# Mixing's value, gate, projection and gated-unit matmuls with activations stationary and 512 weight columns moving

## The chip, the cores and the metric

The kernel runs on one core of one Trainium2 chip. The metric is the device time of one execution in microseconds (us): the median of the runs shown. The span of a profile goes from its first to its last instruction. TensorE multiplies a stationary tile (at most 128 x 128, brought in by a weight load) with a moving tile that streams through it column by column; the result lies in PSUM, which has 8 banks of 128 partitions x 512 float32. VectorE (DVE), ScalarE (ACT) and GpSimd (POOL) do the elementwise work. SyncE (SP) issues the weight transfers.

## The reference

Two layers of a decoder trunk on 256 tokens of width 1024. Each layer is a feed-forward block, a token mixing block and a second feed-forward block, each behind an RMS norm with a modulation (shift, scale, gate) computed from a conditioning vector. The change touches the mixing block alone:

```python
def mixing(h, w_in, ..., w_glu, w_attn_proj, w_out):
    proj = h @ w_in                                   # queries, keys, values, u, gates
    qkv, u, gates = jnp.split(proj, [QKV_COLS, QKV_COLS + SSM_WIDTH], axis=-1)
    ...                                               # o: 24 heads of windowed attention, merged
    y_attn = o.reshape(Bsz, S, ATTN_OUT) @ w_attn_proj
    y_ssm = s5_branch(u, ..., w_glu)                  # scans, gelu, then the gated unit: ga * sigmoid(gb)
    g_attn, g_ssm = jnp.split(jax.nn.sigmoid(gates), 2, axis=-1)
    return (g_attn * y_attn + g_ssm * y_ssm) @ w_out
```

Widths: the values have 1536 columns, the gates 2048, `w_attn_proj` is 512 x 1024, `w_glu` is 512 x 2048, `w_out` 1024 x 1024.

## The kernel before

**Precision.** Every large product is made of three matmuls in the one-pass format `float32r`: each operand is split into a high part and the rest, and `mm3` (line 200) adds high weight times low activation, high times high and low times high into the same PSUM tile. The weights are split on the chip: `split_one` (line 146) takes 1024 columns of a raw weight buffer, ScalarE casts them to the high part `whi` (line 163) and VectorE subtracts to get the low part `wlo` (line 164). Such a piece is called a half; it holds eight 128 x 128 weight tiles. Seven halves can be ready at once (`NHB`), so each cast waits until TensorE has finished with the half seven before it. SyncE reads the raw weights in units of two halves, in a fixed order that `plan_units` and `pack_layer` (line 1238) set; `half` (line 177) hands the next half to the code.

**Layout.** In nearly all products the weight tile is stationary, and the 256 tokens of an activation chunk move: the result has output channels on partitions and tokens along the row. A half is then 8 x 3 = 24 matmuls with 256 moving columns. The values are made the other way round already (`v_quad`, line 1101): the 128 tokens of one token tile are stationary and 256 weight columns move, so the result has tokens on partitions, as attention needs it.

**Mixing** (`mix_sub`, line 866) runs in this order: four column tiles for `u` and two of the first query tiles (`first_block`); query and key pair 0; values for heads 0 to 3 of each group (`v_quad(0)`); pair 1; `v_quad(1)`; pairs 2 and 3 (`qk_pair`); the gates (tiles `gt`, then a tanh on ScalarE into `th`, line 1160); the attention projection (`ap`, line 1167, merged into `th` at line 1168); the gated unit (`gb` and `ga`, line 1177), whose result is merged with the gates in four steps (tanh at line 1180, three VectorE operations at lines 1181 to 1183) and split into `hh` and `hl` (line 1188); and the output projection (`mo`, lines 1200 and 1208), which takes the merged chunks k = 0 to 7 as they come: for its first four column tiles the loop over k is outside. These merges are done for two channel chunks at a time, four times.

**Order.** After each half the code calls `tock` (line 935), which counts slots and emits what `at` put on the slot: the attention of head pair p begins at slot `X0[p]` and goes on in steps of one slot, the 16 state tiles of the scans are spread over slots 5 to 55, and four of the slots prepare the activation `yh`, `yl` of the gated unit. The order on SyncE, GpSimd and ScalarE is that of the code; the order on TensorE and VectorE inside mixing is set when the kernel is built, by a planner that estimates when each instruction can begin. At run time each engine goes through its own list in order.

Of the kernel before, what the change touches and what calls it, by code (L numbers as in the profile page):

```python
# [63 lines left out]
def plan_units():  # L64
    """Order in which the units of weights are read: ('w', i) or ('a', i)."""
# [37 lines left out]
def trunk(ctx, tc, xT, cv, par, ssmp, cst, emat, tbl, wada, wpk, bmat, cmat, out):  # L103
# [37 lines left out]
    def take_ada():  # L141
        """Modulation units whose turn it is."""
# [42 lines left out]
    def several(n):  # L185
        """Halves that are read together."""
# [13 lines left out]
    def mm3(ps, wh, wl, hh, hl, start, stop):  # L200
        T.matmul(ps, lhsT=wh, rhs=hl, start=start, stop=False)  # L201
        T.matmul(ps, lhsT=wh, rhs=hh, start=False, stop=False)  # L202
        T.matmul(ps, lhsT=wl, rhs=hh, start=False, stop=stop)  # L203
# [31 lines left out]
    def ada_unit():  # L235
        """256 columns of silu(c) @ w_ada, one column per partition and element."""
# [57 lines left out]
    def soon(fn):  # L294
        """fn, with its instructions ahead of those that are emitted up to SOON earlier."""
# [16 lines left out]
    def rstd_start():  # L312
        """1 / sqrt(mean of squares + eps), tokens on partitions."""
# [17 lines left out]
    def rstd_spread(ys):  # L331
        """The same on every partition, in PSUM."""
# [10 lines left out]
    def h_tiles(r, scale, shift, hh, hl):  # L343
        """scale * x * r + shift in two parts, chunk by chunk; the chunks take turns in how much of it
        the scalar engine does."""
# [9 lines left out]
        for k in range(KC):  # L355
            hh.append(base.tile([128, S], F32R, name=f"hh{k}", tag=f"hh{k}"))
            hl.append(base.tile([128, S], F32R, name=f"hl{k}", tag=f"hl{k}"))
            b = shift[:, k:k + 1]
            if k % 2:
                A.activation(out=hh[k], in_=t, func=AF.Identity, bias=b)  # L360
            else:
                A.activation(out=t, in_=t, func=AF.Identity, scale=scale[:, k:k + 1], bias=b)
                A.copy(out=hh[k], in_=t)
            n = first(k + 1) if k + 1 < KC else None
            if k % 2:
                stt(hl[k], t, b, hh[k], AD, SU)
            else:
                tt(hl[k], t, hh[k], SU)
# [133 lines left out]
    def table_side(l, pool):  # L502
        """Cosine and sine of each state's angle over time, for the scans of layer l."""
# [27 lines left out]
    def gate_of(sub):  # L531
        """Half the gate."""
# [71 lines left out]
    def first_block(nx, sj, rj):  # L604
        """Five column tiles of a sublayer's input projection. They read scale * x; the rest read the
        normed chunks, which are made meanwhile. What comes back: the banks, 1 / rms, the normed chunks."""
# [5 lines left out]
        def mm(j, w, k):  # L612
            mm3(pss[j][:, :S + 2], w[0][:, k, :], w[1][:, k, :], z[:, k, 0, :], z[:, k, 1, :], k == 0, k == KC - 1)

        hh, hl = [], []
# [13 lines left out]
        for j in range(4):  # L629
            for k in range(5, KC):  # L630
                mm(j, hs[j], k)
            if j == rj:
# [3 lines left out]
                ht = h_tiles(rs, scale, shift, hh, hl)  # L636
# [12 lines left out]
        return pss, rs, hh, hl  # L649

    def first_block_whole(nx, sub):
        """The same for four column tiles, in plain float32."""
        scale, shift, z = nx
        us = [("w", first[sub] + j) for j in range(2)]
        ws = [raw.pop(u).rearrange("p (a b) -> p a b", b=128) for u in us]
        look()
        pss = [bank("b1") for _ in range(4)]

        def mms(ks):
            for j in range(4):  # L660
                for k in ks:
                    T.matmul(pss[j][:, :S + 2], lhsT=ws[j // 2][:, 8 * (j % 2) + k, :], rhs=z[:, k, :],
                             start=k == 0, stop=k == KC - 1)
                if ks[0] == 0 and j == 1:
                    stat_mm()
                    stat["ys"] = rstd_start()
                if ks[0] > 0 and j % 2:
                    finish(us[j // 2])
                    take_ada()

        mms(range(5))
        rps = rstd_spread(stat["ys"])
        rs = tmp.tile([128, S], F32, name="rs", tag="sqa", bufs=1)
        A.copy(out=rs, in_=rps)
        hh, hl = [], []
        for k in h_tiles(rs, scale, shift, hh, hl):
            pass
        mms(range(5, KC))
        look()
        return pss, rs, hh, hl  # L680
# [39 lines left out]
        # bias of each head by distance, for each kind of block of keys: [pq + pk] is that of query  # L720
        # 127 - pq and key pk of the block
# [661 lines left out]
```

## Time and profile before

| what | value |
|---|---|
| median of 3 runs | 1365.01 us (1364.72 to 1365.94) |
| span of the profiled execution | 1361.8 us |
| own time of the profiled execution | not given apart from the span; the median lies 3.2 us above the span |
| TensorE (PE) busy | 1322.1 us, 97% of the span |
| VectorE (DVE) busy | 1098.3 us, 81% |
| ScalarE (ACT) busy | 757.2 us, 56% |
| GpSimd (POOL) busy | 292.6 us, 21% |
| mean granted TensorE clock | 0.993 of 2.4 GHz |

In the rows, PE is a matmul and PEld a weight load. Both are pipelined: the length of one is longer than the time from one start to the next, so the rate of a stream is read from the starts. PEclk is the granted TensorE clock as a share of 2.4 GHz. Inside a group, x is the number of instructions, then come the busy time in us and the mean length of one in ns, and after the second bar the idle time of that engine just before them with what ended it.

### The profile page before, as it was taken

The numbers are of one execution on the slowest core, as the hardware profiler recorded it, in microseconds if no ns is written. First come the engines' busy times: TensorE is split into PE (matmuls) and PEld (weight loads), VectorE is DVE, ScalarE is ACT, GpSimd is POOL, SyncE is SP. The second block draws the span as 40 slices with busy tenths as digits, with TensorE's granted clock in tenths as the row PEclk, the third lists the DMA queues.
The fourth block names the chain that finished last, engine by engine and source line by source line (L and its number), as shares of the span: only waits on it lengthen the run. The fifth ranks groups of instructions, "written<-read, shape, count | busy, mean of one in ns | idle before, by whom it ended". The sixth has DMA issues, their size and how long they took to land.

```text
span 1361.8 us, 26855 instructions
## 1 busy us (share of the span) xinstructions
PE 1322.1 (97%) x11018; PEld 1279.4 (94%) x11018; DVE 1098.3 (81%) x1757; ACT 757.2 (56%) x1162; POOL 292.6 (21%) x356
## 2 busy tenths in 40 slices
PE   4996999999999999999999999999999999999997
PEld 2996999998988999999999999999889999999997
DVE  8866997889899879998769888679889887876552
ACT  5634795645565456677646444454565645654441
POOL 5889691100000000877300000010000000000000
PEclk9997999999999999999999999999999999999999
DMA  9775997556665645998837988656555463586540
GB/s 356 297 289 175 369 347 274 187 193 207 219 234 219 217 153 170 347 370 321 279 124 291 351 316 333 247 174 227 173 199 198 163 220 128 182 307 217 186 155 32
DMA packets 48837, 321.60 MB, mean 236 GB/s; under 512 B 6048, under 2 KB 6432, under 8 KB 12746
## 3 DMA queue, kind: packets, MB, share of 16 engines
q1 hardware_dynamic: 41704, 296.24, 59.8%
q0 software_dynamic: 7008, 23.64, 5.4%
q8 instruction: 86, 1.41, 0.4%
q14 instruction: 37, 0.30, 0.1%
q10 hardware_dynamic: 2, 0.00, 0.0%
HBM read 310.38 MB, written 9.48 MB: 235 GB/s over the span
## 4 chain that ended last, share of the span: by engine, by line
PE 86%; POOL 6%; DVE 3%; issue 2%; ACT 1%; DMA 1%; DVEq 0%; POOLq 0%; ACTq 0%
PE pc L203 8%; PE pc L201 8%; PE pc L202 8%; PE fo L201 6%; PE fo L202 6%; PE fo L203 6%; PE qk L201 4%; PE qk L202 3%; PE qk L203 3%; PE gt L201 3%; PE gt L202 2%; PE gt L203 2%; PE b L201 2%; PE bu L949 2%; PE b L203 2%; PE b L202 2%
## 5 line engine op out<-in xcount | busy, mean ns | idle before, releaser
L164 DVE TENSOR_TENSOR wlo<-raw,whi 128x1024 fp32r<-128x1024 f32 x416 | 515.5, 1257 | 93.2 <-ACT whi L163 92.3
L163 ACT CAST whi<-raw 128x1024 fp32r<-128x1024 f32 x416 | 427.0, 1047 | 220.2 <-PE fo L202 71.3
L201 PE MATMUL pc<-hl,whi 128*128 128x256 f32 x1200 | 338.4, 282 | 8.7 <-ACT whi L163 8.7
L203 PE MATMUL pc<-hh,wlo 128*128 128x256 f32 x1200 | 338.2, 282 | 3.6 <-DVE wlo L164 3.6
L202 PE MATMUL pc<-hh,whi 128*128 128x256 f32 x1200 | 338.2, 282 | 0.0
L201 PEld LDWEIGHTS pc<-hl,whi 128*128 128x128 f32 x1200 | 226.6, 189 | 8.9 <-ACT whi L163 8.9
L203 PEld LDWEIGHTS pc<-hh,wlo 128*128 128x128 f32 x1200 | 226.5, 189 | 4.1 <-DVE wlo L164 4.1
L202 PEld LDWEIGHTS pc<-hh,whi 128*128 128x128 f32 x1200 | 226.7, 189 | 0.0
L201 PE MATMUL fo<-al,whi 128*128 128x256 f32 x704 | 197.7, 281 | 0.2 <-DVE al L341 0.2
L202 PE MATMUL fo<-ah,whi 128*128 128x256 f32 x704 | 197.8, 281 | 0.0
L203 PE MATMUL fo<-ah,wlo 128*128 128x256 f32 x704 | 197.7, 281 | 0.0
L247 DVE CUSTOM_DVE_ANT_0 raw<-raw,cb 128x1024 f32<-128x1024 f32 x144 | 182.2, 1300 | 7.4 <-DMA raw<-wada 7.1
L201 PEld LDWEIGHTS fo<-al,whi 128*128 128x128 f32 x704 | 132.6, 188 | 0.4 <-DVE al L341 0.4
L202 PEld LDWEIGHTS fo<-ah,whi 128*128 128x128 f32 x704 | 132.7, 188 | 0.0
L203 PEld LDWEIGHTS fo<-ah,wlo 128*128 128x128 f32 x704 | 132.7, 188 | 0.0
L201 PE MATMUL qk<-hl,whi 128*128 128x256 f32 x352 | 102.4, 292 | 0.0
L202 PE MATMUL qk<-hh,whi 128*128 128x256 f32 x352 | 99.1, 282 | 0.0
L203 PE MATMUL qk<-hh,wlo 128*128 128x256 f32 x352 | 98.7, 281 | 0.0
L389 POOL TENSOR_SCALAR tr<-tp 128x256 f32<-128x256 f32 x32 | 45.6, 1424 | 146.8 <-ACT tp L509 146.1
L883 POOL DMA_DIRECT2D tab<-tab x32 | 17.4, 545 | 267.8 <-DVE pq L276 171.3
L201 PE MATMUL gt<-hl,whi 128*128 128x256 f32 x256 | 74.7, 292 | 0.0
L201 PEld LDWEIGHTS qk<-hl,whi 128*128 128x128 f32 x352 | 66.1, 188 | 7.1 <-issue 4.7
(220 smaller groups left out, 2915.4 us busy)
## 6 DMA issues: line engine op xcount, KB each, us to landing
raw<-wpk SPq DMA_DIRECT2D x208, 1024.0 KB, 5.4
raw<-wada SPq DMA_DIRECT2D x72, 1024.0 KB, 6.8
tab<-tb POOLq DMA_DIRECT2D x32, 256.0 KB, 5.7
tab<-tab POOLq DMA_DIRECT2D x32, 256.0 KB, 3.6
bt<-wd POOLq DMA_DIRECT2D x8, 640.0 KB, 6.2
xt<-xT SPq DMA_DIRECT2D x1, 1024.0 KB, 4.9
bT<-bmat POOLq DMA_DIRECT2D x2, 512.0 KB, 4.8
out<-xt SPq DMA_DIRECT2D x4, 256.0 KB, 2.2
```

The source lines that it names most:

```text
L163: A.copy(out=hi.rearrange("p a b -> p (a b)"), in_=src)
L164: low.tensor_sub(out=lo.rearrange("p a b -> p (a b)"), in0=src, in1=hi.rearrange("p a b -> p (a b)"))
L201: T.matmul(ps, lhsT=wh, rhs=hl, start=start, stop=False)
L202: T.matmul(ps, lhsT=wh, rhs=hh, start=False, stop=False)
L203: T.matmul(ps, lhsT=wl, rhs=hh, start=False, stop=stop)
L247: V.tensor_tensor_reduce(out=wj, in0=wj, in1=cb, scale=1.0, scalar=0.0, op0=ALU.mult, op1=ALU.add, accum_out=m[:, c:c + 1])
L389: G.tensor_scalar(out=o, in0=i, scalar1=s1, scalar2=s2, op0=op0, op1=op1)
L883: G.dma_start(out=tabs[s], in_=tabd[l][s])
L949: T.matmul(ps[:, i * S:i * S + S], lhsT=w[r, i, q, :], rhs=u[q][r], start=n == 0, stop=n == 2, tile_position=(32 * jj, 0))
```

## The change

Each activation chunk now lies in one tile of shape [128, 2, 256], the low part first (`hx`, `ax`, `ux`, `yx`, `ox`, `mx` in place of the pairs `hh`/`hl` and so on); the matmuls that keep their form read the same parts in the same order through it. The values, the gates, the attention projection and the gated unit are made by `block512`: the activations are stationary, 128 tokens at a time, and 512 weight columns move; a block takes two PSUM banks, one for each token tile, over its n / 2 halves. `pack_layer` packs the weights so that a half holds two chunks of the contraction times 512 columns. The merge with the gates is then done with tokens on partitions, twice for 512 channels and two token tiles, and TensorE transposes the merged tiles back to channels on partitions (16 transposes of 128 x 128 in a layer) before they are split out of PSUM. All values are made between query and key pairs 0 and 1, and the attention of pair 1 begins at slot 24, not 19. `first_block_whole`, which was not used, is gone; `mm2` is new and not used.

```diff
-X0 = 12, 19, 31, 37
+X0 = 12, 24, 31, 37
...
+    def mmt(ps, x, t, wh, wl, start, stop):
+        sl = slice(128 * t, 128 * t + 128)
+        T.matmul(ps, lhsT=x[:, 0, sl], rhs=wh, start=start, stop=False)
+        T.matmul(ps, lhsT=x[:, 1, sl], rhs=wh, start=False, stop=False)
+        T.matmul(ps, lhsT=x[:, 1, sl], rhs=wl, start=False, stop=stop)
+
+    def block512(name, x, n, tock):
+        ps = [bank(name) for t in range(2)]
+        for h in range(n // 2):
+            wh, wl = (w.rearrange("p (a b) c -> p a (b c)", a=2) for w in half())
+            for t in range(2):
+                for k in (2 * h, 2 * h + 1):
+                    mmt(ps[t], x[k], t, wh[:, k % 2], wl[:, k % 2], k == 0, k == n - 1)
+            tock()
+        return ps
...
-            def v_quad(b):
-                t = mp.tile([128, 3, 2, 256], F32, name="vt", tag="vt", bufs=2)
...
+            def v_all():
                 for g in range(3):
+                    ps = block512("v", hx, KC, tock)
+                    for t in range(2):
+                        for b in range(2):
+                            A.copy(out=vv[b][:, g, t], in_=ps[t][:, 256 * b:256 * b + 256])
...
             qk_pair(0)
-            v_quad(0)
+            v_all()
             qk_pair(1)
-            v_quad(1)
             qk_pair(2)
             qk_pair(3)
...
-            for dp in range(4):
+            for db in range(2):
                 for gi in range(2):
+                    for t, ps in enumerate(block512("gt", hx, KC, tock)):
+                        th[gi, db, t] = tslots.pop(0)
+                        A.activation(out=th[gi, db, t], in_=ps, func=AF.Tanh, scale=0.5)
+            for db in range(2):
+                for t, ps in enumerate(block512("ap", [ox[:, k] for k in range(4)], 4, tock)):
+                    stt(th[0, db, t], th[0, db, t], 1.0, ps, AD, MU)
+            mx = []
+            for db in range(2):
+                pb = block512("gb", yx, 4, tock)
+                pa = block512("ga", yx, 4, tock)
+                for t in range(2):
+                    tb = mp.tile([128, 512], F32, name="tb", tag="lg", bufs=4)
+                    A.activation(out=tb, in_=pb[t], func=AF.Tanh, scale=0.5)
+                    stt(tb, tb, 1.0, pa[t], AD, MU)
+                    stt(th[1, db, t], th[1, db, t], 1.0, tb, AD, MU)
+                    stt(th[0, db, t], th[1, db, t], 0.5, th[0, db, t], MU, AD)
+                for n in range(2):
+                    pt = bank("mt")
                     for j in range(2):
...
+                        for t in range(2):
+                            T.transpose(pt[:, S * j + 128 * t:S * j + 128 * t + 128],
+                                        th[0, db, t][:, 256 * n + 128 * j:256 * n + 128 * j + 128], ident)
                     for j in range(2):
...
+                        mx.append(part_tile(4 * db + 2 * n + j))
+                        split_act(pt[:, S * j:S * j + S], mx[-1][:, 1], mx[-1][:, 0])
```

## Rows read from the trace of the kernel before

**Rows 1.** The page, busy time of each engine over the whole span.

```profile
PE 1322.1 (97%) x11018; PEld 1279.4 (94%) x11018; DVE 1098.3 (81%) x1757; ACT 757.2 (56%) x1162; POOL 292.6 (21%) x356
```

**Rows 2.** Stretches of mixing in layers 0 and 1 (values to gated unit); its gates alone.

```profile
core 0: us, PE busy (x) PEld busy (x) DVE busy (x) ACT busy (x) POOL busy (x), PEclk, DMA share, GB/s
263.87:487.35 223.48, 223.40 (x1868) 204.91 (x1868) 202.12 (x354) 119.73 (x185) 10.58 (x17) 1.00 0.62 215
385.51:450.72 65.21, 65.21 (x561) 59.77 (x559) 61.69 (x112) 37.74 (x58) 1.62 (x3) 1.00 0.63 220
918.58:1139.18 220.60, 220.52 (x1867) 204.37 (x1867) 192.98 (x334) 121.32 (x188) 10.96 (x17) 1.00 0.57 196
```

**Rows 3.** Groups by line, the first of each three equal matmul groups that change.

```profile
L201 PE MATMUL gt<-hl,whi 128*128 128x256 f32 x256 | 74.7, 292 | 0.0
L1113 PE MATMUL v<-whi,hl 128*128 128x256 f32 x192 | 55.6, 290 | 0.0
...
L201 PE MATMUL ap<-ol,whi 128*128 128x256 f32 x64 | 18.3, 286 | 0.0
L201 PE MATMUL ga<-yl,whi 128*128 128x256 f32 x64 | 18.0, 282 | 0.0
L201 PE MATMUL gb<-yl,whi 128*128 128x256 f32 x64 | 18.0, 281 | 0.0
```

**Rows 4.** Timeline of TensorE in the values, full clock (start us, length us, instruction).

```profile
264.33 0.29 PE L1113 MATMUL v<-whi,hl 128*128 128x256 f32 x1
...
266.94 0.28 PE L1114 MATMUL v<-whi,hh 128*128 128x256 f32 x1
```

**Rows 5.** A stretch of the first feed-forward block at half clock: windows view.

```profile
117.80:120.30 2.50, 2.50 (x13) 2.50 (x13) 2.50 (x3) 2.15 (x5) 2.33 (x3) 0.50 1.08 380
```

**Rows 6.** Timeline of TensorE at its start.

```profile
117.81 0.41 PE L201 MATMUL pc<-hl,whi 128*128 128x256 f32 x1
...
119.09 0.41 PE L201 MATMUL pc<-hl,whi 128*128 128x256 f32 x1
```

**Rows 7.** Timeline of TensorE: transposes of attention behind a matmul of the gates.

```profile
401.26 0.28 PE L203 MATMUL gt<-hh,wlo 128*128 128x256 f32 x1
401.38 1.04 PE L1050 MATMUL pt<-cs,lg 128*128 128x128 f32 x8
```

**Rows 8.** Timeline of the weight loads of the same transposes.

```profile
401.28 0.90 PEld L1050 LDWEIGHTS pt<-cs,lg 128*128 128x128 f32 x8
```

**Rows 9.** Groups by line: merges, and copies and splits out of PSUM and SBUF.

```profile
L1136 ACT COPY qk<-qk 128x256 f32<-128x256 f32 x24 | 9.0, 374 | 29.1 <-PE qk L203 29.1
L1117 ACT COPY vt<-v 128x512 f32<-128x512 f32 x12 | 7.0, 583 | 2.8 <-PE v L1115 2.8
L341 DVE TENSOR_TENSOR hl<-thb,hh 128x256 fp32r<-128x256 f32 x16 | 6.1, 422 | 3.8 <-ACT hh L340 3.8
...
L279 DVE SCALAR_TENSOR_TENSOR thb<-thb 128x512 f32<-128x512 f32 x8 | 5.5, 692 | 0.3
L279 DVE SCALAR_TENSOR_TENSOR thb<-thb,tb 128x512 f32<-128x512 f32 x8 | 5.5, 692 | 0.3
...
L279 DVE SCALAR_TENSOR_TENSOR tb<-tb,ga 128x512 f32<-128x512 f32 x8 | 5.4, 680 | 0.4 <-PE ga L203 0.4
...
L341 DVE TENSOR_TENSOR ol<-po,oh 128x256 fp32r<-128x256 f32 x8 | 3.4, 420 | 1.0 <-ACT oh L340 0.8
L340 ACT CAST oh<-po 128x256 fp32r<-128x256 f32 x8 | 2.9, 366 | 0.0
```

**Rows 10.** Timeline of TensorE where the output projection of layer 0 begins.

```profile
487.35 0.28 PE L201 MATMUL mo<-hl,whi 128*128 128x256 f32 x1
```

**Rows 11.** Timeline of VectorE there: the last merge of layer 0.

```profile
486.59 2.36 DVE L164 TENSOR_TENSOR wlo<-raw,whi 128x1024 fp32r<-128x1024 f32 x2 [0.49 <-ACT whi L163]
488.87 0.68 DVE L279 SCALAR_TENSOR_TENSOR tb<-tb,ga 128x512 f32<-128x512 f32 x1
```

**Rows 12.** Timeline of VectorE: the gated unit's last input in layer 0.

```profile
462.71 0.42 DVE L1005 TENSOR_TENSOR yl<-yy,yh 128x256 fp32r<-128x256 f32 x1
```

**Rows 13.** Timeline of VectorE: the same in layer 1.

```profile
1113.83 0.42 DVE L1005 TENSOR_TENSOR yl<-yy,yh 128x256 fp32r<-128x256 f32 x1
```

**Rows 14.** Timeline of TensorE: first matmul of the gated unit in layer 0.

```profile
464.31 0.28 PE L201 MATMUL gb<-yl,whi 128*128 128x256 f32 x1
```

**Rows 15.** Timeline of TensorE: the same in layer 1.

```profile
1116.15 0.28 PE L201 MATMUL gb<-yl,whi 128*128 128x256 f32 x1
```

**Rows 16.** The page, transfers by issue: the attention's bias (last: median us to landing).

```profile
bt<-wd POOLq DMA_DIRECT2D x8, 640.0 KB, 6.2
```

More of the change, by code (lines that the diff above doesn't have):

```diff
@@ L341, in split_act, with part_tile, h_tiles @@
         V.tensor_sub(out=lo, in0=src, in1=hi)
-    def h_tiles(r, scale, shift, hh, hl):
+    def part_tile(k):
+        return base.tile([128, 2, S], F32R, name=f"hx{k}", tag=f"hx{k}")
+    def h_tiles(r, scale, shift, hx):
         def first(k):
@@ L648, in first_block @@
             split_one()
[L649 to L680, printed above, removed]
+        return pss, rs, hx
     def first_sublayer():
@@ L753, in first_sublayer @@
             t = boot.tile([128, S], F32, name="hb", tag="hb", bufs=2)
[L754 removed]
+            hx.append(part_tile(k))
             A.activation(out=t, in_=xr[:, k, :], func=AF.Identity, scale=sc[:, k:k + 1], bias=sh[:, k:k + 1])
[L756 to L758 removed]
+            A.copy(out=hx[k][:, 1], in_=t)
+            late.append((hx[k], t))
             if k == 0:
@@ L947, in ssm_in @@
                 for i in range(2):
-                    for n, (w, u) in enumerate(((bh, ul), (bh, uh), (bl, uh))):
-                        T.matmul(ps[:, i * S:i * S + S], lhsT=w[r, i, q, :], rhs=u[q][r], start=n == 0, stop=n == 2,
+                    for n, (w, u) in enumerate(((bh, 0), (bh, 1), (bl, 1))):
+                        T.matmul(ps[:, i * S:i * S + S], lhsT=w[r, i, q, :], rhs=ux[q][r, u], start=n == 0, stop=n == 2,
                                  tile_position=(32 * jj, 0))
@@ L1138, in qk_pair @@
                 qk[p] = t
+            vv = [mp.tile([128, 3, 2, 256], F32, name="vt", tag="vt", bufs=2) for b in range(2)]
             qk_pair(0)
-            v_quad(0)
+            v_all()
             qk_pair(1)
-            v_quad(1)
             qk_pair(2)
@@ L1150, in mix_sub @@
                 tslots += [big[:, n] for n in range(3)]
-            for dp in range(4):
+            for db in range(2):
                 for gi in range(2):
-                    ps = bank("gt")
-                    for j in range(2):
-                        wh, wl = half()
-                        for k in range(KC):
-                            mm3(ps[:, j * S:j * S + S], wh[:, k, :], wl[:, k, :], hh[k], hl[k], k == 0, k == KC - 1)
-                        tock()
-                    t = tslots.pop(0)
-                    A.activation(out=t, in_=ps, func=AF.Tanh, scale=0.5)
-                    th[gi, dp] = t
@@ L1258, in pack_layer, with wide @@
         cols(t, 36 + j)
-    def vq(b):
-        for g in range(NG):
-            n = 24 + 4 * g + 2 * b
-            seq.append(t[:, n:n + 2].reshape(16, 128, 128))
+    def wide(t, n):
+        seq.append(t[:, n:n + 4].reshape(-1, 128, 128))
     def qkp(p):
@@ L1270, in pack_layer @@
     qkp(0)
-    vq(0)
+    for g in range(NG):
+        wide(t, 24 + 4 * g)
     qkp(1)
-    vq(1)
     qkp(2)
     qkp(3)
-    for dp in range(4):
+    for db in range(2):
         for gi in range(2):
-            for j in range(2):
-                cols(t, 40 + 8 * gi + 2 * dp + j)
+            wide(t, 40 + 8 * gi + 4 * db)
     t = tiles(a["w_attn_proj"][l])
-    for d in range(KC):
-        cols(t, d)
+    for db in range(2):
+        wide(t, 4 * db)
     t = tiles(a["w_glu"][l])
-    for dp in range(4):
+    for db in range(2):
         for h in (1, 0):
-            for j in range(2):
-                cols(t, 8 * h + 2 * dp + j)
+            wide(t, 8 * h + 4 * db)
     t = tiles(a["w_out"][l])
```

150 lines of the change are left out of this document (52 added, 98 removed).

## The prediction, made before the changed kernel ran

> **What bounds the kernel now.** I read the page's busy times first: TensorE has matmuls in flight for 97% of the span, VectorE is next with 81% [rows 1]. Such an average hides stages, so the windows view of mixing comes next. From the first value matmul to the end of the gated unit TensorE is covered for all but 0.08 us, in both layers, at full clock, while VectorE is busy for 202.1 of 223.5 us in layer 0 and 193.0 of 220.6 in layer 1 [rows 2]. So in the stretch that the change touches, time is the number of matmuls times the step from one start to the next. A busy TensorE is not one at its peak, so the timeline gives the step: from 264.33 to 266.94 there are 22 steps, 2.61 / 22 = 0.1186 us for 256 moving columns [rows 4]. VectorE is close behind: over the gates of layer 0 it is busy 61.7 of 65.2 us [rows 2].
>
> **What 256 columns cost, and 512 should.** The nearest rows on either side are these. At half clock (PEclk 0.50 [rows 5], the 1.2 GHz level) the same kind of matmul, also with a weight load each, steps 1.28 / 6 = 0.2133 us [rows 6], which is 256 / 1.2 GHz and nothing more. At full clock, streaming alone would be half of that, 0.1067; the step is 0.0119 longer. In the half-clock row the stream is far longer than a weight load of 128 columns, which repeats every (0.90 - 0.14) / 7 = 0.109 us in front of the transposes (0.14 being my allowance for the last load's own latency) [rows 8]; at full clock load and stream take the same time. That suggests that the extra 0.0119 belongs to the meeting of the two and shrinks when the stream takes twice as long, as 512 columns at full clock do. Bounds for one 512-column matmul: below, streaming alone, 0.2133; above, two steps of today, 0.2372, if the extra is a rate per column. Between them stands 0.2133 + 0.0119 = 0.2252, if the extra is a fixed price per matmul. I take 0.219, the middle of 0.2133 and 0.2252: the half-clock row is the nearest one in shape (same format, same load, stream as long as it will be), but its front end has twice the time for each column. The saving is 0.2372 - 0.219 = 0.0182 us for each pair replaced.
>
> The Trainium skill, "TensorE: Matmul & The Clock Gate", section "Back-to-back issue gap", speaks against the change: at full clock it gives N / 2.4 GHz plus 2.5 ns, so a pair of 256 columns would cost 218.4 ns and one of 512 costs 215.8, an estimate of 2.5 us saved over the 960 pairs below, which is less than the transposes cost. The trace disagrees for 256 columns with a load each: 118.6 ns instead of 109.2. With today's step from the rows and the page's 215.8 for the new one, the saving would be 20.5 us and the time 1353.0.
>
> **The change, part by part.**
>
> *Matmuls.* The values have 3 x 192 matmuls, the gates 3 x 256, projection 3 x 64, gated unit 2 x 3 x 64 [rows 3]: 576 + 768 + 192 + 384 = 1920 of 256 columns in both layers, which become 960 of 512. Saved: 960 x 0.0182 = **17.5 us**; with the bounds 0 to 22.9, all of it on the path, since TensorE waits for nothing there.
>
> *Transposes.* 32 in all. Those of attention begin 0.12 us after the last gate matmul and step (1.04 - 0.28) / 7 = 0.109 us [rows 7]. Added: 32 x 0.109 = **3.5 us**, on TensorE and so on the path.
>
> *The tail of the merge.* Today the output projection starts at 487.35 [rows 10] with six of eight chunks ready; the last merge starts at 488.87, behind two weight splits of 2.36 us together [rows 11]. Afterwards only chunks 0 to 3 are ready: 4 x 4 x 3 = 48 matmuls of 0.1186, or 5.7 us, plus eight transposes, 0.9: 6.6 us of work. Chunk 4 needs 1.5 us until the first merge (as today), six merge operations of 0.680 + 2 x 0.692 for each token tile, 4.1, four transposes, 0.45, a cast and a subtraction out of PSUM, 0.37 + 0.42 (as attention's `oh` and `ol` [rows 9]), and some 0.2 of handing over: 7.1 us. So 0.5 us is left bare, and each further weight split of 1.2 us that stands between adds to it. Bounds per layer: 0 and 6.2 (the whole 5.65 until the merges are done, and the 0.5, if the transposes stand in TensorE's list ahead of the 48 matmuls). I take 1.5, so **3.0 us** for both layers. Chunks 5 to 7 follow 0.4 us apart and TensorE takes 1.4 for each. The same merge for the first 512 channels has a whole 11 us of gated unit to lie beside.
>
> *The scans' end.* The gated unit needs `yl` of the last states, which is ready 1.2 us before the unit starts in layer 0 and 1.9 in layer 1 [rows 12 to 15]. By then TensorE will be (144 + 192 + 48) x 0.0182 = 7.0 us earlier in each layer. The new order asks for the last chunk only after 15 matmuls of the unit, 3.3 us. If VectorE finishes no earlier than today, TensorE waits 7.0 - 1.2 - 3.3 = 2.5 us in layer 0 and 1.8 in layer 1; if it uses its free time (21.4 and 27.6 us in the two stretches [rows 2]), nothing. Bounds 0 and 4.3; I take **2.0**. Until then the seven halves that may be split ahead cover VectorE's bursts.
>
> *Moved or changed at no price.* All values come before pair 1, and pair 1's attention moves by five slots with its 32 small VectorE and ScalarE operations; TensorE's own work is the same and the projection, its first reader, is 17 slots after its end. GpSimd's load of pair 2's bias is issued five slots later, three slots (72 x 0.1186 = 8.5 us) ahead of use, and takes 6.2 to land [rows 16]; the table loads stand behind it on GpSimd's queue. Pair 3 already has two slots only. If that cover is gone, VectorE waits 1 or 2 us once in each layer, inside its free time. SyncE moves the same units, in another packing. ScalarE copies the values as 12 pieces of 0.374 us in place of 6 of 0.583, 1.0 us more in a layer [rows 9], beside its 46% free time [rows 2]. Splitting out of PSUM costs no more than out of SBUF (0.420 against 0.422 us [rows 9]). A block holds two of the eight PSUM banks for four slots, where one was held for two; attention may get its banks later, which the slack of its slots covers. The joined low and high tiles change addresses, not operations.
>
> **Sum.** -17.5 + 3.5 + 3.0 + 2.0 = -9.0. The profiled span is 1361.8, and the median of the runs 3.2 above it; the difference is taken off the median: 1365.0 - 9.0 = **1356.0 us**.
>
> **Rivals.**
>
> *The extra is a fixed price per matmul.* For: it is what a pair of instructions, load and matmul, would cost in any front end. Against: the half-clock row has the same pair and shows no extra [rows 6]. Then one of 512 takes 0.2252 and the change saves 960 x 0.0119 = 11.4; less 8.5 at most (TensorE is earlier by less, so 2.0 shrinks to nothing): 1365.0 - 11.4 + 6.5 = 1360.1, up to 1362.1.
>
> *The columns themselves are slow (the other side).* If at full clock a float32r column takes 0.1186 / 256 = 0.463 ns however many there are, nothing is saved, and the transposes and the tail in the output projection are added: 1365.0 + 6.5 = 1371.5, slower. For: the half-clock row cannot exclude a reading rate that only full clock reaches. Against: no row shows such a rate limit. It decides from 0.230 us for one 512-column matmul upwards, where 960 x 0.007 pays just the 6.5.
>
> *The gain is lost in waits.* VectorE does as much as before in less time; over the gates of layer 0 its 61.7 us would have only 65.2 - 192 x 0.0182 = 61.7. If its list falls behind, the scans' end costs all its 4.3, and if the transposes are in front of the output projection's first matmuls, the tail costs 12.4: 1365.0 - 17.5 + 3.5 + 4.3 + 12.4 = 1367.7; with one of the two, about 1358 to 1365. For: both orders are fixed by a planner's estimates. Against: today no matmul of mixing waits.
>
> **How the numbers follow.** Of this kernel a measurement can tell about 0.2%, 2.7 us, from no change: faster means below 1362.3, slower above 1367.7. Forecast 0.58 (1349 to 1361, all faster); fixed price 0.15 (0.08 faster, 0.07 same); slow columns 0.12 (0.01 same, 0.11 slower); lost in waits 0.15 (0.05 faster, 0.07 same, 0.03 slower). Together 0.71 faster, 0.15 same, 0.14 slower. The bounds reach from 1365.0 - 22.9 + 3.5 = 1345.6 to 1371.5; the range 1349 to 1366 leaves out the slow columns and the corner where streaming is free and nothing waits.
>
> **What would show it.** In the profile after: the step of the 512-column matmuls, read from the starts in the timeline (0.219 right, 0.225 or 0.237 the rivals); 32 new transposes of 0.11; the wait of the output projection or its transposes on VectorE's merge, 1 to 2 us a layer; the gated unit's wait on `yl`; VectorE's share in the gates near 98%. The length of values, gates, projection and unit should fall by 8 to 9 us a layer before waits. A step above 0.23, or waits of more than 10 us on VectorE, would make the prediction wrong.

## The result, and the profile after

The changed kernel takes **1389.51 us** (median of 4 runs, 1388.5 to 1391.26) where the kernel before, run beside it, takes 1364.87 (4 runs, 1363.96 to 1365.94): a ratio of 1.018, interval 1.0166 to 1.0194. It is 24.6 us slower; 9 us faster was forecast, in a range that ended at 1366. The profiled execution after has a span of 1389.2 us and took 1391.26, the longest of the four; the spans of the two profiles lie 27.4 us apart. One run of the kernel `late` below took 1611.78 us at a mean granted clock of 0.756 and is left out of its time.

Ahead of all detail stands the page's line of busy times after, which answers to [rows 1].

```profile
PE 1335.6 (96%) x10090; PEld 1241.1 (89%) x10090; DVE 1096.7 (79%) x1757; ACT 759.6 (55%) x1174; POOL 296.1 (21%) x356
```

TensorE has 928 matmuls fewer (960 less the 32 transposes), and yet it is busy 13.5 us longer. VectorE's sum has hardly changed. So there are two things to find: why fewer matmuls keep TensorE busy for longer, and where the other half of the time goes. The waits view of TensorE answers the second; its columns are what waited and for whom, the sum in us, how often, and the longest.

```profile
PE mt L1157 <- DVE thb L309: 13.7, 4, 4.2
```

This line is new: four of the new transposes (`mt`, line 1157) wait 13.7 us in all for VectorE's merge. The windows view shows the stages: gates of layer 0, then from the first matmul of the gated unit to the end of the output projection in each layer, then the block behind it, then three short stretches.

```profile
core 0: us, PE busy (x) PEld busy (x) DVE busy (x) ACT busy (x) POOL busy (x), PEclk, DMA share, GB/s
...
387.39:452.96 65.57, 65.57 (x368) 50.15 (x367) 61.20 (x111) 38.14 (x59) 1.84 (x4) 1.00 0.61 213
...
466.15:523.27 57.12, 50.21 (x306) 45.08 (x305) 35.40 (x58) 24.92 (x42) 0.00 (x0) 0.94 0.39 145
523.27:541.47 18.20, 18.20 (x154) 18.20 (x153) 14.80 (x43) 9.27 (x19) 0.00 (x0) 1.00 0.40 141
1130.80:1189.24 58.44, 51.69 (x306) 46.28 (x305) 35.38 (x55) 25.12 (x42) 0.00 (x0) 0.91 0.34 126
...
497.00:502.40 5.40, 5.40 (x28) 5.40 (x26) 0.25 (x1) 0.28 (x1) 0.00 (x0) 0.50 0.20 79
...
1144.86:1147.90 3.04, 3.04 (x9) 2.46 (x10) 0.45 (x1) 0.00 (x0) 0.00 (x0) 0.50 0.23 92
...
1162.90:1168.30 5.40, 5.40 (x28) 5.40 (x26) 0.21 (x1) 0.31 (x1) 0.00 (x0) 0.50 0.18 76
```

For comparison, the same view of the kernel before: gated unit with output projection in layer 0, and the block behind it.

```profile
464.31:510.14 45.83, 45.83 (x387) 45.83 (x386) 34.65 (x54) 24.24 (x41) 0.00 (x0) 1.00 0.51 178
510.14:528.33 18.19, 18.19 (x155) 18.19 (x154) 15.53 (x45) 9.86 (x20) 0.00 (x0) 1.00 0.45 146
```

Three things are to be seen. The gates take 65.57 us where they took 65.21 [rows 2], with 192 fewer starts: 3.5 us were to be saved there. Gated unit and output projection take 57.12 and 58.44 us, against 45.83 (in layer 1 the same): 11.3 and 12.6 us longer, together 23.9 of the 27.4. And inside these are three stretches at a granted clock of 0.50, the 1.2 GHz level, which together last 5.40 + 3.04 + 5.40 = 13.8 us. Half of that, 6.9 us, is lost; it is some 7.5 us with the edges of the stretches, which these windows leave out.

The timeline of TensorE after shows what comes before them (start us, length us, instruction, idle time before it and what ended that).

```profile
466.06 0.39 PE L214 MATMUL gb<-whi,yx 128*128 128x512 f32 x1
...
470.27 0.40 PE L214 MATMUL ga<-whi,yx 128*128 128x512 f32 x1
...
477.07 0.39 PE L216 MATMUL ga<-wlo,yx 128*128 128x512 f32 x1
480.12 0.44 PE L1157 MATMUL mt<-cs,thb 128*128 128x128 f32 x2 [2.66 <-DVE thb L309]
480.31 0.48 PE L214 MATMUL gb<-whi,yx 128*128 128x512 f32 x1
...
492.05 0.40 PE L216 MATMUL ga<-wlo,yx 128*128 128x512 f32 x1
496.70 0.69 PE L1157 MATMUL mt<-cs,thb 128*128 128x128 f32 x2 [4.25 <-DVE thb L309]
497.04 0.56 PE L202 MATMUL mo<-hx,whi 128*128 128x256 f32 x1
```

Two transposes stand in TensorE's list directly behind the last `ga` matmul of each block. (In the code all eight of a block come there; the planner moved the other six back, behind 20 matmuls of `gb` or 19 of `mo`.) Behind them stands work that is ready: `gb` of the second block starts as soon as the first two transposes are through (480.31), and the output projection's matmuls on chunks 0 to 3 as soon as the other two are (497.04). TensorE goes through its list in order, so it stands idle for 2.66 and 4.25 us. Layer 1 has the same two, 2.75 and 4.01 us. What the transposes wait for is in the timeline of VectorE.

```profile
474.60 2.36 DVE L164 TENSOR_TENSOR wlo<-raw,whi 128x1024 fp32r<-128x1024 f32 x2 [3.46 <-ACT whi L163]
476.88 1.38 DVE L309 SCALAR_TENSOR_TENSOR tb<-tb,ga 128x512 f32<-128x512 f32 x2
478.17 1.28 DVE L309 SCALAR_TENSOR_TENSOR thb<-thb,tb 128x512 f32<-128x512 f32 x2
479.38 1.29 DVE L309 SCALAR_TENSOR_TENSOR thb<-thb 128x512 f32<-128x512 f32 x2
...
490.16 3.49 DVE L164 TENSOR_TENSOR wlo<-raw,whi 128x1024 fp32r<-128x1024 f32 x3
493.56 1.28 DVE L309 SCALAR_TENSOR_TENSOR tb<-tb,ga 128x512 f32<-128x512 f32 x2
494.76 1.28 DVE L309 SCALAR_TENSOR_TENSOR thb<-thb,tb 128x512 f32<-128x512 f32 x2
495.96 1.28 DVE L309 SCALAR_TENSOR_TENSOR thb<-thb 128x512 f32<-128x512 f32 x2
```

Weight splits come first (three of 1.2 us in the second place). Then the six merge operations take the two token tiles in turn, so even the first tile's merge is done only after five of the six. Here one late merge operation holds up all of TensorE. ScalarE is held in its turn: its cast of a transposed chunk stands ahead of the weight casts that follow, as its timeline shows at the second place.

```profile
502.12 0.37 ACT L370 CAST hx<-mt 128x256 fp32r<-128x256 f32 x1 [9.32 <-PE mt L1157]
```

The step of the 512-column matmuls comes from the timeline above: 18 steps from 466.06 to 470.27, 4.21 / 18 = **0.234 us**. From the starts of all of them, holes left out, the means are 0.2327 (values), 0.2323 (gates), 0.2332 (projection), 0.2339 (`gb`) and 0.2345 (`ga`): some 0.004 less than the two steps of 0.1186 that one replaces [rows 4], not 0.018.

### The profile page after: what moved, and what is told of

The parts are those of the page before. It is cut to its first block, busy times and chain, and to the rows that moved or that the text cites. A ratio compares the mean times of both kernels' runs of the same rounds, so it can differ in the third digit from the quotient of the medians.

```text
span 1389.2 us, 25027 instructions
## 1 busy us (share of the span) xinstructions
PE 1335.6 (96%) x10090; PEld 1241.1 (89%) x10090; DVE 1096.7 (79%) x1757; ACT 759.6 (55%) x1174; POOL 296.1 (21%) x356
## 4 chain that ended last, share of the span: by engine, by line
PE 89%; POOL 6%; DVE 2%; issue 1%; ACT 0%; DMA 0%; DVEq 0%; POOLq 0%
PE pc L204 9%; PE pc L202 9%; PE pc L203 9%; PE fo L203 6%; PE fo L204 6%; PE fo L202 6%; PE qk L202 3%; PE qk L204 3%; PE qk L203 3%; PE gt L214 2%; PE gt L215 2%; PE gt L216 2%; PE b L231 2%; PE bu L946 2%; PE b L233 2%; PE b L232 2%
## 5 line engine op out<-in xcount | busy, mean ns | idle before, releaser
L202 PE MATMUL pc<-hx,whi 128*128 128x256 f32 x1200 | 339.0, 283 | 9.2 <-ACT whi L163 9.2
L204 PE MATMUL pc<-hx,wlo 128*128 128x256 f32 x1200 | 338.8, 283 | 3.7 <-DVE wlo L164 3.7
L203 PE MATMUL pc<-hx,whi 128*128 128x256 f32 x1200 | 338.8, 283 | 0.0
L202 PEld LDWEIGHTS pc<-hx,whi 128*128 128x128 f32 x1200 | 227.3, 190 | 9.4 <-ACT whi L163 9.4
L204 PEld LDWEIGHTS pc<-hx,wlo 128*128 128x128 f32 x1200 | 227.1, 189 | 3.9 <-DVE wlo L164 3.9
L203 PEld LDWEIGHTS pc<-hx,whi 128*128 128x128 f32 x1200 | 227.3, 189 | 0.0
L203 PE MATMUL fo<-ax,whi 128*128 128x256 f32 x704 | 197.9, 281 | 0.0
L204 PE MATMUL fo<-ax,wlo 128*128 128x256 f32 x704 | 197.8, 281 | 0.0
L202 PE MATMUL fo<-ax,whi 128*128 128x256 f32 x704 | 197.6, 281 | 0.0
L203 PEld LDWEIGHTS fo<-ax,whi 128*128 128x128 f32 x704 | 132.7, 188 | 0.0
L204 PEld LDWEIGHTS fo<-ax,wlo 128*128 128x128 f32 x704 | 132.7, 188 | 0.0
L202 PEld LDWEIGHTS fo<-ax,whi 128*128 128x128 f32 x704 | 132.6, 188 | 0.0
L202 PE MATMUL qk<-hx,whi 128*128 128x256 f32 x352 | 102.0, 291 | 0.0
L203 PE MATMUL qk<-hx,whi 128*128 128x256 f32 x352 | 99.1, 282 | 0.0
L204 PE MATMUL qk<-hx,wlo 128*128 128x256 f32 x352 | 99.1, 283 | 0.0
```

The source lines that it names most:

```text
L202: T.matmul(ps, lhsT=wh, rhs=x[:, 0], start=start, stop=False)
L203: T.matmul(ps, lhsT=wh, rhs=x[:, 1], start=False, stop=False)
L204: T.matmul(ps, lhsT=wl, rhs=x[:, 1], start=False, stop=stop)
```

## The experiments

The leading theory ("theory 1") was that the time goes into the place of the transposes in TensorE's list. "Theory 2" was that the form with 512 columns itself costs the time; the expectations set further rivals against theory 1. Every ratio is against the kernel before on the same chip.

**Transposes later (`late`).** The transposes of the first 512 channels are emitted behind the second block's `gb`, those of the second behind the output projection's chunks 0 to 3.

```diff
+            def turn(db):
                 for n in range(2):
                     pt = bank("mt")
...
             for db in range(2):
                 pb = block512("gb", yx, 4, tock)
+                if db:
+                    turn(0)
                 pa = block512("ga", yx, 4, tock)
...
             for k in range(KC):
+                if k == 4:
+                    turn(1)
                 for j in range(4):
```

> The changed kernel with one thing moved: the transposes and splits of the first 512 channels are emitted between gb and ga of the second block, those of the second 512 after the output projection's chunks 0 to 3, so that TensorE has 24 to 48 matmuls to do before it reaches them. Theory 1 (the loss is TensorE standing at transposes whose merge is not done, 13.7 us, and the half clock that follows the longest two stands): 1367 to 1371 us, no wait of a transpose over 1 us, the output projection steps 0.119 us throughout. Theory 2 (the 512-column form itself costs the time, in steps or in the small matmuls between): no better than 1383 us, since the number of 512-column matmuls is the same.

Measured: 1380.13 us (median of three), ratio 1.0107 (1.0092 to 1.0123). The move wins back 9.4 us, so the place matters; but 1367 to 1371 is missed by as much. The waits view of `late` says what is left at the transposes and a wait that the kernel after does not have.

```profile
PE mt L1150 <- DVE thb L309: 3.8, 2, 2.1
...
PE b L231 <- DVE z L309: 3.2, 2, 1.6
```

And its windows (gated unit to output projection in layer 0, the block behind it, the same in layer 1):

```profile
465.31:515.08 49.77, 47.71 (x309) 42.88 (x308) 32.44 (x52) 22.30 (x38) 0.00 (x0) 1.00 0.40 144
515.08:535.20 20.12, 18.51 (x153) 18.09 (x152) 17.70 (x49) 11.95 (x23) 0.00 (x0) 1.00 0.52 180
1124.51:1174.41 49.90, 47.79 (x309) 42.96 (x308) 32.39 (x49) 22.43 (x38) 0.00 (x0) 1.00 0.35 124
1174.41:1194.53 20.12, 18.50 (x153) 18.08 (x152) 17.71 (x49) 11.95 (x23) 0.00 (x0) 1.00 0.52 179
```

The clock is 1.00 throughout. But the next block, 18.20 us long after the change and 18.19 before it, now takes 20.12: VectorE does 49 operations in it, not 43, and 1.6 us of the 1.9 are a wait for one of them. Taken later, the merge's work collides with the input of the next block.

**Two of 256 in place of one of 512 (`cols256`).** All else as after.

```diff
-        T.matmul(ps, lhsT=x[:, 0, sl], rhs=wh, start=start, stop=False)
-        T.matmul(ps, lhsT=x[:, 1, sl], rhs=wh, start=False, stop=False)
-        T.matmul(ps, lhsT=x[:, 1, sl], rhs=wl, start=False, stop=stop)
+        for c in (slice(0, 256), slice(256, 512)):
+            T.matmul(ps[:, c], lhsT=x[:, 0, sl], rhs=wh[:, c], start=start and c.start == 0, stop=False)
+            T.matmul(ps[:, c], lhsT=x[:, 1, sl], rhs=wh[:, c], start=False, stop=False)
+            T.matmul(ps[:, c], lhsT=x[:, 1, sl], rhs=wl[:, c], start=False, stop=stop and c.start > 0)
```

> The changed kernel with each 512-column matmul made as two of 256 columns into the two halves of the same bank, 1920 in all; layout, order of the weights, merge and transposes as changed. Theory 1: 512 columns step 0.2325 us against 2 x 0.1186, so this is slower than the changed kernel by 960 x 0.0047 = 4.5 us, 1394 us, with the same waits of the transposes. Theory 2: faster than the changed kernel, 1375 us or less.

Measured: 1385.76 us, ratio 1.0155 (1.0141 to 1.0169). Against 1394 a miss: without the long matmuls the kernel is not slower than after but 3.7 us faster. The waits view of TensorE has the four stands again, now of 2.75 us each.

```profile
PE mt L1158 <- DVE thb L310: 11.0, 4, 2.7
```

Half clock follows the second stand of each layer here too; the windows view has it in layer 1:

```profile
1158.00:1160.00 2.00, 2.00 (x12) 2.00 (x11) 0.00 (x0) 0.00 (x0) 0.00 (x0) 0.52 0.16 61
1160.00:1162.00 2.00, 2.00 (x14) 2.00 (x13) 0.00 (x0) 0.00 (x0) 0.00 (x0) 0.63 0.00 0
```

That is half clock for 2 x 2 x (0.48 + 0.37) = 3.4 us; with the like in layer 0 some 3.4 us are lost, where the kernel after loses 6.9 by the windows above. Waits shorter by 2.7 and 3.5 less at half clock are 6.2 of the 6.8 us that lie between the two spans (1389.2 and 1382.4). So on balance the 512 columns save nothing elsewhere, and the loss at the transposes comes with either form.

**Values alone (`values`).** The kernel before, with all values between pairs 0 and 1 (`X0` 12, 24, 31, 37) and 512 weight columns moving in them.

```diff
-X0 = 12, 19, 31, 37
+X0 = 12, 24, 31, 37
...
+            def v_all():
+                for g in range(3):
+                    ps = [bank("v") for t in range(2)]
...
             qk_pair(0)
-            v_quad(0)
+            v_all()
             qk_pair(1)
-            v_quad(1)
```

> The kernel before with the values alone made by 512-column matmuls, all of them between pairs 0 and 1, and the attention of pair 1 at slot 24; gates, projection, gated unit and merge as before, no transposes. Theory 1: 288 matmuls of 512 save 288 x 0.0047 = 1.4 us and the moved attention costs nothing: 1363 to 1365 us. Theory 2: 288 of the 960, so a share of the loss, 5 us or more: 1370 us.

**The order alone (`order`).** The kernel before, with its 256-column values in the new order.

```diff
-X0 = 12, 19, 31, 37
+X0 = 12, 24, 31, 37
...
             qk_pair(0)
             v_quad(0)
-            qk_pair(1)
             v_quad(1)
+            qk_pair(1)
...
-    qkp(1)
     vq(1)
+    qkp(1)
```

> The kernel before with the order of the change alone: both value quads between pairs 0 and 1, the attention of pair 1 at slot 24, matmuls of 256 columns, no merge changed. If the order costs what the stretch from the first query to the gates showed with 256 columns (2.4 us in layer 0, 1.1 in layer 1): 1368 us. If that came from the two banks that a block holds, or from the joined tiles: 1365 us.

Measured: `values` 1365.30, ratio 1.0002 (0.9993 to 1.0011); `order` 1365.53, ratio 1.0005 (0.9996 to 1.0013). The new order costs nothing in the total that can be told from zero, as predicted. Nor does making 288 pairs of matmuls into one each give anything in the total, where 5.2 us had been counted. Theory 2's 1370 for `values` did not come either.

**The streams by themselves (`steps`).** A kernel of matmul streams alone; the rest of the computation is left out. Each stream has 48 matmuls with a weight load each (four stationary tiles in turn) unless the name says otherwise, at the end two while VectorE and ScalarE are busy.

```diff
+    def phase(name, s, m, n, cols=128, count=48, one=False):
+        ps = pp.tile([128, 512], F32, tag="ps", name=name)
+        for i in range(count):
+            T.matmul(ps[:cols, :n], lhsT=s[:, 0 if one else i % 4, :cols], rhs=m[:, i % 2, :n], start=i == 0, stop=i == count - 1)
...
+    phase("q512", st, mv, 512)
+    phase("q384", st, mv, 384)
+    phase("q256", st, mv, 256)
+    phase("q128", st, mv, 128)
...
+    ps = phase("b256", stb, mvb, 256)
...
+    phase("busy512", st, mv, 512, count=72)
```

> No part of the computation: streams of matmuls alone, each with its weight load, at full clock; the output is the input. float32r with 512, 384, 256 and 128 moving columns and nothing else running, 512 with a stationary tile of 32 columns, bfloat16 with 512 and 256, then float32r 512 and 256 beside VectorE subtractions and ScalarE casts of 1024 columns. If a float32r column has a rate of its own: about 0.232 for 512, 0.175 for 384, 0.118 for 256, no shorter with a stationary tile of 32, the same quiet and busy, and bfloat16 near 0.216. If the extra over 0.2133 comes from the weight load: 0.216 with a stationary tile of 32. If it comes from the other engines' traffic: 0.216 for 512 when nothing else runs, 0.232 when they do.

The groups by line of `steps` (q is float32r, b is bfloat16, q512c has stationary tiles of 32 columns, busy is the one beside VectorE and ScalarE; count, busy us, mean ns of one):

```profile
L37 PE MATMUL busy<-mv,st 128*128 128x512 f32 x72 | 16.6, 391 | 0.0
...
L37 PE MATMUL q512c<-mv,st 128*32 128x512 f32 x48 | 11.3, 394 | 0.0
...
L37 PE MATMUL q<-mv,st 128*128 128x512 f32 x48 | 11.0, 389 | 0.0
...
L37 PE MATMUL q<-mv,st 128*128 128x384 f32 x48 | 8.5, 335 | 0.0
L37 PE MATMUL q<-mv,st 128*128 128x256 f32 x48 | 5.9, 283 | 0.0
L37 PE MATMUL q<-mv,st 128*128 128x128 f32 x48 | 5.5, 274 | 0.0
L37 PE MATMUL b<-mvb,stb 128*128 128x256 bf16 x48 | 5.4, 273 | 0.0
```

A stream is busy for all its steps and the length of the last one: (11.0 - 0.389) / 47 = 0.226 us for 512 columns, (8.5 - 0.335) / 47 = 0.174 for 384, (5.9 - 0.283) / 47 = 0.1195 for 256. From one to the next that is 0.41 ns a column, which is 2.4 GHz, and in each a remainder of 0.013: **a fixed price for a matmul**, the rival whose 0.2252 the prediction worked out. In bfloat16 256 columns take (5.4 - 0.273) / 47 = 0.109. 128 columns in float32r take 0.111, about what a weight load takes [rows 8]. VectorE and ScalarE add little: (16.6 - 0.391) / 71 = 0.228. Nor does a weight load of 32 columns take the extra away: (11.3 - 0.394) / 47 = 0.232, so the load is not what makes it.

**The same with the kernel's own sequence (`steps2`, `steps3`).** As `steps`, with the loop of `block512` over stationary and moving tiles and two accumulations; `steps2` quiet (q), beside transfers (d), and beside VectorE and ScalarE (e); `steps3` with true high and low parts, quiet (q) and beside all three at once (f).

```diff
-    def phase(name, s, m, n, cols=128, count=48, one=False):
+    def phase(name, cols, reps=4):
...
+            for h in range(2):
+                for t in range(2):
+                    for k in range(2):
+                        for x, w in ((0, 0), (1, 0), (1, 1)):
```

> No part of the computation: the changed kernel's own sequence of a block (stationary tiles low, high, high of joined activation tiles, moving high, high, low weights of 512 or as two of 256 columns, two banks in turn), first with nothing else running, then beside transfers of 1 MB into SBUF, then beside VectorE and ScalarE. Alone the simple stream stepped 0.227 for 512 and 0.120 for 256, the kernel 0.2325 and 0.1186. If the sequence of operands makes the difference: 0.2325 in all three. If the transfers: 0.227, 0.2325, 0.227. If neither: 0.227 throughout, and the difference lies in the accumulation next to other work on PSUM.

> No part of the computation: the block sequence of before with real high and low parts as operands, quiet, then beside transfers, VectorE and ScalarE all at once. If values or all the traffic together make the difference between 0.227 (alone) and 0.2325 (in the kernel): 0.2325 in the first or the second. If not, 0.227 in both, and what makes the difference stays open.

Groups by line of `steps2`:

```profile
L43 PE MATMUL d<-wt,hx 128*128 128x256 f32 x192 | 23.2, 283 | 0.0
...
L43 PE MATMUL d<-wt,hx 128*128 128x512 f32 x96 | 21.9, 389 | 0.0
L43 PE MATMUL e<-wt,hx 128*128 128x512 f32 x96 | 21.9, 389 | 0.0
L43 PE MATMUL q<-wt,hx 128*128 128x512 f32 x96 | 21.9, 389 | 0.0
```

(21.9 - 0.389) / 95 = 0.226 and (23.2 - 0.283) / 191 = 0.120 in every case, and in `steps3` the same again. So neither the sequence nor the data, the transfers or the other engines make the 0.2323 to 0.2345 of the kernel. What does is open.

**Without the transposes (`noturn`).** After, with the 32 transposes left out: the split reads parts of the merged tiles directly, so tokens and channels are not exchanged for the output projection. All other work is as after.

```diff
-                    pt = bank("mt")
-                    for j in range(2):
-                        for t in range(2):
-                            T.transpose(pt[:, S * j + 128 * t:S * j + 128 * t + 128],
-                                        th[0, db, t][:, 256 * n + 128 * j:256 * n + 128 * j + 128], ident)
                     for j in range(2):
                         mx.append(part_tile(4 * db + 2 * n + j))
-                        split_act(pt[:, S * j:S * j + S], mx[-1][:, 1], mx[-1][:, 0])
+                        split_act(th[0, db, j][:, S * n:S * n + S], mx[-1][:, 1], mx[-1][:, 0])
```

> The changed kernel without its 32 transposes: the parts of the merge are split straight from the merged tiles, so the turning back to channels on partitions is left out; every other instruction and the merge stay. Theory 1 (TensorE stands at the transposes, and they stand early in its list): 1389.5 - 13.7 of waits - 3.5 of transposes - about 4 of half clock = 1368 us or less, and no wait of the output projection over 1 us, since its first 48 matmuls cover the merge. Rival (the merge itself is late: six VectorE operations of 0.69 us with nothing to lie beside): TensorE waits for the split of chunk 4 in place of the transposes, 1378 us or more.

Measured: 1366.71 us, ratio 1.0013 (1.0004 to 1.0022): what theory 1 had, and not the 1378 or more of its rival. Its window from the gated unit to the end of the output projection in layer 0:

```profile
465.82:511.34 45.52, 45.52 (x290) 41.12 (x289) 34.97 (x57) 24.90 (x42) 0.00 (x0) 1.00 0.51 182
```

That is 0.3 us less than before, and 11.6 less than after. So 1389.51 - 1366.71 = 22.8 us hang on the transposes. The rest of the change is 1.7 us slower than the kernel before it, where the prediction had 15.5 faster (17.5 less 2.0).

**Transposes of what is ready (`ready`).** After, with the 32 transposes in their place, but reading chunks of the residual, which are ready long before, and not the merged tiles. The output projection so gets other values; the merge is still made.

```diff
-                                        th[0, db, t][:, 256 * n + 128 * j:256 * n + 128 * j + 128], ident)
+                                        xs[4 * db + 2 * n + j][:, 128 * t:128 * t + 128], ident)
```

> The changed kernel with its 32 transposes reading chunks of the residual x, which are long there, in place of the merged tiles: the merge is still made but its result isn't used, so the output projection multiplies other data. The transposes and their splits out of PSUM stay, the wait for the merge goes. Theory 1 (bare transposes cost their 0.109 us, the rest of the loss is waiting for the merge and the half clock behind it): the kernel without transposes, 1366.7, + 3.5 = 1370 us, no wait at the transposes, the output projection at full clock. Rival (the transposes cost by being in TensorE's stream, switching back and forth or holding PSUM banks): 1380 us or more.

Measured: 1370.47 us, ratio 1.0036 (1.0024 to 1.0049), as theory 1 had it. Its windows, gated unit to output projection in both layers:

```profile
466.30:513.31 47.01, 47.01 (x306) 42.51 (x305) 35.23 (x58) 25.05 (x42) 0.00 (x0) 1.00 0.49 178
1120.85:1167.86 47.01, 47.01 (x306) 42.51 (x305) 35.14 (x55) 25.16 (x42) 0.00 (x0) 1.00 0.44 157
```

The same 306 matmuls take 47.01 us in place of 57.12 and 58.44, at full clock, with no idle time. With `noturn` this splits the loss: the transposes themselves cost 1370.47 - 1366.71 = 3.8 us (2 x 1.49 in the windows), waiting for the merge 1389.51 - 1370.47 = 19.0. In the profiles the latter is 10.1 + 11.4 = 21.5 us, of which 13.7 are the four stands and 6.9 the half clock behind them.

**Later still, with more work in front (`late2`).** As `late`, with six column tiles over chunks 0 to 3 first (72 matmuls in front of the last transposes, not 48), and each column tile finished before the next.

```diff
-            hs = several(4)
-            pss = [bank("mo") for _ in range(4)]
+            hs = several(6)
+            pss = [bank("mo") for _ in range(6)]
...
+            turn(1)
             for d in range(KC):
-                if d < 4:
+                if d < 6:
```

> The kernel with late transposes, with six column tiles of the output projection over chunks 0 to 3 ahead of the second transposes (72 matmuls, 8.5 us) and each column tile finished before the next, so that VectorE gets the first of them early. Theory 1: the waits at the transposes (3.8 us in the late kernel) and of the next block on VectorE (3.5) go; left are the transposes, 3.5, and what the order of values and attention costs: 1368 to 1372 us. Rival (the loss is in the matmuls): 1380 us as the late kernel.

Measured: 1376.45 us, ratio 1.0085 (1.0072 to 1.0099): the wait at the transposes is gone, but 1368 to 1372 is missed. Its windows in layer 0 (gated unit to output projection, the block behind):

```profile
465.68:513.79 48.11, 47.51 (x307) 42.75 (x307) 32.89 (x55) 22.76 (x38) 0.00 (x0) 1.00 0.40 142
513.79:533.47 19.68, 18.22 (x152) 18.01 (x151) 17.26 (x45) 11.52 (x22) 0.00 (x0) 1.00 0.53 201
```

1.1 us are left in the first against `ready`, and 1.5 in the second, where TensorE now waits 1.5 us for VectorE at the next norm's sum of squares (`stat`). Each cure moves the wait one stage on. How much of it belongs to VectorE's list and how much to ScalarE's was not tried.

## Why the prediction was wrong

- **The tail of the merge (3.0 us) is the term that failed**: 13.7 us of stands and 6.9 of half clock took its place. Two steps were wrong. The bounds of 0 to 6.2 us a layer even named the case ("if the transposes stand in TensorE's list ahead of the 48 matmuls"), with a chance of 0.15 shared with another wait; it came, in both layers. And "the same merge for the first 512 channels has a whole 11 us of gated unit to lie beside" was false: that holds only if the transposes stand behind those matmuls in the list, and they stand in front of them, so the first block cost 2.66 and 2.75 us too. The chain was estimated at 7.1 us for chunk 4; what TensorE saw of it was 4.25 and 4.01.
- **The clock was no term at all.** The kernel before has stretches at 0.50 [rows 5], and the prediction used one for the step, but did not ask what TensorE had done before them. Behind the stands of 4.25 and 4.01 us the granted clock was 0.50 for 5.4 us each, behind one of 2.75 for 3.0, and behind the one of 2.66 it stayed at 1.00.
- **The step (17.5 us saved) was mis-sized.** 0.219 was the middle between the half-clock row and a fixed price. The streams alone show the fixed price (0.226), and the kernel more than that, 0.2323 to 0.2345, beyond the 0.230 from which the prediction's rival of slow columns decides. A step above 0.23 and waits of more than 10 us on VectorE were the prediction's own signs of being wrong, and both came. By these steps 960 pairs save about 4.5 us (4.1 by these means, 5.2 by the sum of all starts below). The half-clock rows misled: they step by 0.2133, with nothing beyond the columns, and so do not show the 0.013 that the streams show at full clock. The Trainium skill, "TensorE: Matmul & The Clock Gate", section "Back-to-back issue gap", gives N / 2.4 GHz plus 2.5 ns as the gap of single matmuls at full clock; the bfloat16 stream agrees (0.109 for 256 columns), the float32r streams do not (0.013 in place of 0.0025).
- **Even 4.5 us did not show**: `noturn` is at 1.0013, and the gates are 0.36 us longer than before in layer 0. The saving came, but TensorE's small matmuls gave it back, which the prediction had put at nothing ("TensorE's own work is the same"). Summed from each start to the next over whole traces, the matmuls that change take 5.2 us less in `noturn` than before. The 256 matmuls of the attention's logits (`lg`) take 20.8 us in place of 17.5, and the 128 of the scans (`yps`) 22.7 in place of 20.1. The groups by line show the logits before and after (`noturn` has 22.3 too):

```profile
L1020 PE MATMUL lg<-qk 64*128 64x128 f32 x256 | 18.6, 285 | 0.0
L1015 PE MATMUL lg<-qk 64*128 64x128 f32 x256 | 22.3, 286 | 0.0
```

  The timeline of TensorE shows one such place in the gates of layer 0, before (first line) and after:

```profile
406.29 1.16 PE L1020 MATMUL lg<-qk 64*128 64x128 f32 x16
407.66 1.16 PE L1015 MATMUL lg<-qk 64*128 64x128 f32 x8
409.73 1.16 PE L1015 MATMUL lg<-qk 64*128 64x128 f32 x8
```

  Before, the 16 begin two at a time, 0.111 us from one pair to the next; after, they stand in two groups of eight that begin one at a time, 0.112 us apart, with two `yps` and a 512-column matmul between the groups. The order is the planner's. No run holds it fixed, so that it alone makes `noturn` miss the saving is not shown: the 256-column `order` has 19.1 for the logits and 19.9 for `yps`, and `cols256` 19.1 and 20.5. The latter are 4.0 less together than after the change, which is about what `cols256` was expected to lose by its steps and did not.
- **The scans' end (2.0 us) cost nothing.** In layer 0 VectorE starts the last `yx` part at 466.15, after the unit's own start at 466.06, and TensorE does not wait, since the unit asks for the last chunk only later. But the case that was priced did not come: the unit was to start 7.0 us earlier, and it starts later than before (466.06 against 464.31 [rows 14]). So the 2.0 us were not put to the test.
- **Transposes (3.5 us)** measured 3.8, and the moved values and attention, the copies and banks cost nothing in the total that can be told (`order`, 1.0005; `values`, 1.0002). These prices were right; only the small matmuls above were not.
- **The rival "the gain is lost in waits"** was the nearest: it came with its upper wait and the slow step together, and with a half clock that it did not have. The worked 1367.7 was too low by 21.8 us: 13.0 of the saving that did not come, 8.2 of further waits and clock (20.6 against 12.4), the transposes of the first block among them; less the 4.3 of the scans' end that was not lost; the 4.9 that remain are about the 4.5 that did not show.

## What to carry to other kernels

A step that turns data on TensorE puts the engine that makes the data into TensorE's list: before pricing it, ask where it will stand in that list, what ready work stands behind it, and when the last of a chain of merge operations will be done; a wait there is paid for in idle time and, behind some of the stands here, again at half clock. Adding work later in the list cures it only as far as VectorE then has nothing due itself, so look at the next block's first wait as well. Count on longer matmuls for the fixed price per matmul alone, and measure that price in the format in question, at full clock. Then look in the new list for small matmuls that ran two at a time before and no longer do.

## What the runs showed of the hardware that was not expected

- In float32r a matmul costs 0.013 us beyond its columns at 2.4 GHz (512, 384 and 256 columns: 0.226, 0.174, 0.1195); in bfloat16 256 columns take 0.109, 0.002 beyond them. A stationary tile of 32 columns does not shorten the 512 (0.232), so the price goes with the format and not with the length of the weight load.
- The same stand did not always cost the clock: after the change 2.66 us left it at 1.00 and 2.75 us brought 3.04 us at 0.50. In `cols256` all four stands were 2.75 us; half clock is seen behind the second of each layer, and none behind the first. The runs do not show what decides it.
- In the kernel 512 columns take 0.2323 to 0.2345 us, alone 0.226, with the same sequence, data and traffic. This stays open.
- Logits of 64 rows, the two heads of a pair in turn, begin two at a time: 16 take 1.16 us. Eight that stand by themselves take 1.16 us as well.
